# Layer 2's decay matrix: maxima broadcast by a load from DRAM scratch and masked on GpSimd, gate logarithms taken by tokens

## The chip, the core and the metric

The kernel runs on one core of a Trainium2 chip. The metric is device time in microseconds (us) of one execution; a lower number is better. TensorE (PE in the profile, with its weight loads as PEld) multiplies matrices, VectorE (DVE) and ScalarE (ACT) work on elements, GpSimd (POOL) does the same more slowly and issues some DMAs, SyncE (SP) issues the weight DMAs. Each engine takes its own instructions strictly in order; where one waits for a semaphore, everything behind it on that engine waits too.

## The reference, cut to what matters

A decoder trunk of two layers for 256 tokens of width 1024, in float32: layer 1 of the program is sparse attention, layer 2 is an mLSTM mixer with 8 heads (key width 128, value width 256). Layer 2's core, with input gate `i_pre` and forget gate `log_f` per token and head:

```
i_pre = gi + gate_b[0];  log_f = log_sigmoid(gf + gate_b[1])
b = cumsum(log_f);  log_d[j,s] = b[j] - b[s] + i_pre[s]  for s <= j, else -inf
m_j = max over s of log_d[j,s]
S = (q k^T) * exp(log_d - m_j);  num = S v;  den = sum of S
h = num / max(|den|, exp(-m_j))
```

The reference works in chunks of 64 tokens. The kernel uses the whole-sequence form of the same thing: with F the running sum of log_f, G = i_pre - F and M the running maximum of G, the decay factor of a key s and a query j is exp(G[s] - M[j]), and the floor of the denominator is exp(-(M + F)).

## The kernel before, in words

Keys of a decay matrix lie on the 128 partitions. For each head `DT[:, h]` has 384 columns: 256 for the first 128 keys against all queries, and 128 for the second 128 keys against the second 128 queries. In both, one 128x128 square is triangular.

Most of the program is the streamed projection of tokens: a weight block of 128x1024 is loaded by SP into one of 10 `raw` buffers (L86), ScalarE rounds it to a high part `wh` (L164), VectorE subtracts to get the low part `wl` (L169), and TensorE makes three products of each (hi·hi, lo·hi, hi·lo). There are 6 pairs of `wh`/`wl`, so the splits run some five blocks ahead of TensorE. In layer 2 a `tok_unit` of 512 columns takes four blocks (L548 to L550, 12 matmuls of 512 columns for each), a `ws_unit` two (L1611 to L1613, 24 matmuls of 256 columns for each).

The order of instructions on each engine is set by a scheduler that models the engines when the program is built; a region marked high priority goes ahead of other work as soon as the model finds its inputs ready. What is `pin`ned stays in the order of the text.

Layer 2 begins with the gate columns: 16 columns of a product (8 input gates, 8 forget gates, tokens on partitions) are copied to `GT` (L1240). Then, at high priority:

- four TensorE transposes bring `GT` to 8 rows of 256 tokens (L1332), and VectorE adds the biases (L1333, L1334);
- the log-sigmoid is computed on these 8x256 rows by three ScalarE functions and some VectorE operations (L1335 to L1343), then the running sum and maximum by scans (L1344, L1346), and -M is put in `nM` in two float32r parts (L1347 to L1349);
- two transposes bring G to columns (L1351), copied to `GF` (L1352);
- for every head, a matmul of a selector column with `nM` broadcasts -M over the partitions (L1357), two bf16 matmuls add the triangular mask (L1358, L1359), and two ScalarE exponentials with bias G write `DT` out of the PSUM bank (L1360, L1361).

Later the floor exp(-(M + F)) is made on rows (L1363 to L1365) and transposed by two more TensorE instructions (L1368).

The convolutions over q and k follow: each `conv_unit` is one `ws_unit`, a ScalarE pass out of PSUM (L1380), six VectorE taps (L1385) and a SiLU (L1387); by a rule in the text the SiLUs are issued behind the last decay exponential. `rows` shares its buffer with `QK`, into which the SiLUs write. Heads (L1392 on) use `DT` much later.

Of the kernel before, what the change touches and what calls it, by code (L numbers as in the profile page):

```python
# [23 lines left out]
class Kernel:  # L24
# [225 lines left out]
    def setup(self):  # L250
# [53 lines left out]
        self.identr = self.T(self.p1, [P, P], F32R)
        nc.vector.tensor_copy(self.identr, self.ident)
        nc.vector.tensor_copy(self.selh[0:8], self.ident[0:8, 0:8])

    def late_constants(self):
# [3 lines left out]
        m32 = self.T(self.p1, [P, P])  # L312
        g.memset(m32, 0.0)
        g.affine_select(m32, m32, pattern=[[1, P]], compare_op=OP.is_ge, fill=-1e30, base=0, channel_multiplier=-1)
        g.tensor_copy(self.mask, m32)
        g.tensor_copy(self.identb, self.ident)

    def small_loads(self):
        nc, t = self.nc, self.t
        self.first_small = [(self.pca[:, 32:89], t["second"])]  # L320
        self.small = [(self.bif, t["gate_b"]), (self.pcb, t["mixer"]), (self.compress, t["compress"])]
# [770 lines left out]
    def turn(self):  # L1092
# [146 lines left out]
        for a in range(2):  # L1239
            nc.vector.tensor_copy(GT[:, a], bs[a][:, 256:272])  # L1240
# [41 lines left out]
    def layer2(self):  # L1282
# [18 lines left out]
        mask, identb, selh = self.mask, self.identb, self.selh  # L1301
# [19 lines left out]
        rows = self.T(p2, [8, 9, SEQ], tag="QK")  # L1321
        gi, xf, e, u, sp, d, ones, Fc, M = [rows[:, n] for n in range(9)]
        nM = self.T(p2, [P, 384], F32R)
        GF = self.T(p2, [P, 2, 2, 8])
        g.memset(ones, 1.0)
        g.memset(nM.bitcast(F32), 0.0)
        bg, bt = self.bank(2), self.bank(3)
        with self.tc.high_priority():
            for a in range(2):
# [6 lines left out]
            nc.scalar.activation(e, e, AF.Exp, scale=-1.0)
            nc.vector.tensor_scalar(u, e, 1.0, None, op0=OP.add)
            nc.scalar.activation(sp, u, AF.Ln)
            nc.vector.scalar_tensor_tensor(d, u, -1.0, e, op0=OP.add, op1=OP.subtract)
            nc.vector.reciprocal(u, u)  # L1340
            nc.vector.tensor_tensor(d, d, u, op=OP.mult)
            nc.vector.tensor_sub(sp, sp, d)
            nc.vector.scalar_tensor_tensor(sp, xf, 0.0, sp, op0=OP.min, op1=OP.subtract)  # L1343
            nc.vector.tensor_tensor_scan(Fc, ones, sp, 0.0, OP.mult, OP.add)  # L1344
            nc.vector.tensor_sub(gi, gi, Fc)
            nc.vector.tensor_tensor_scan(M, ones, gi, 0.0, OP.mult, OP.max)  # L1346
            nc.vector.tensor_scalar(nM[0:8, 0:SEQ], M, -1.0, None, op0=OP.mult)  # L1347
            nc.vector.scalar_tensor_tensor(nM[32:40, 0:SEQ], M, -1.0, nM[0:8, 0:SEQ].bitcast(F32), op0=OP.mult, op1=OP.subtract)
            nc.vector.tensor_copy(nM[0:40, SEQ:384], nM[0:40, P:SEQ].bitcast(F32))  # L1349
            for a in range(2):  # L1350
                nc.tensor.transpose(bt[:, 8 * a : 8 * a + 8], gi[:, a * P : a * P + P], ident[:8, :8])  # L1351
            nc.vector.tensor_copy(GF[:, 0].rearrange("p a h -> p (a h)"), bt[:, 0:16])  # L1352
        DT = self.T(p2, [P, 8, 384], tag="DT")
        with self.tc.high_priority():
            for h in range(8):
                b = self.bank(2 + h % 2)
                nc.tensor.matmul(b[:, 0:384], selh[:, h : h + 1].to_broadcast([P, P]), nM, start=True, stop=False, skip_group_check=True)  # L1357
                nc.tensor.matmul(b[:, 0:P], identb, mask, start=False, stop=False, skip_group_check=True)  # L1358
                nc.tensor.matmul(b[:, SEQ:384], identb, mask, start=False, stop=True, skip_group_check=True)  # L1359
                nc.scalar.activation(DT[:, h, 0:SEQ], b[:, 0:SEQ], AF.Exp, bias=GF[:, 0, 0, h : h + 1])  # L1360
                last = nc.scalar.activation(DT[:, h, SEQ:384], b[:, SEQ:384], AF.Exp, bias=GF[:, 0, 1, h : h + 1])  # L1361
        v_unit(2, 2)
        nc.vector.tensor_tensor(M, M, Fc, op=OP.add)  # L1363
        nc.vector.tensor_scalar(M, M, -88.0, None, op0=OP.max)
        last = nc.scalar.activation(M, M, AF.Exp, scale=-1.0)  # L1365
        b = self.bank(2)
        for a in range(2):
# [328 lines left out]
```

## Time and profile before

| what | value |
|---|---|
| median of 3 runs | 427.54 us (427.27 to 427.9) |
| span of the profiled execution | 425.8 us |
| own time of the profiled execution | not listed apart from its span; the median lies 1.74 us above the span |
| PE busy | 415.7 us, 98% of the span |
| DVE, ACT, POOL busy | 353.7 us (83%), 272.0 us (64%), 82.1 us (19%) |
| granted TensorE clock | 0.999 |
| DMA | 94.54 MB, mean 222 GB/s |

The span runs from the first to the last instruction. A row of a timeline gives the start, the duration, the engine, the line, the operation and its operands (output first), and in brackets how long the engine was idle before and what ended it. Matmuls are pipelined: a 256-column matmul lasts 0.28 us but the next starts 0.12 us later, so what an instruction costs TensorE is read from the distance of starts. A row of windows gives busy time of each engine in a stretch, then the granted clock, the share of DMA engines busy and GB/s.

### The profile page before, as it was taken

The numbers are of one execution on the slowest core, as the hardware profiler recorded it, in microseconds if no ns is written. First come the engines' busy times: TensorE is split into PE (matmuls) and PEld (weight loads), VectorE is DVE, ScalarE is ACT, GpSimd is POOL, SyncE is SP. The second block draws the span as 40 slices with busy tenths as digits, with TensorE's granted clock in tenths as the row PEclk, the third lists the DMA queues.
The fourth block names the chain that finished last, engine by engine and source line by source line (L and its number), as shares of the span: only waits on it lengthen the run. The fifth ranks groups of instructions, "written<-read, shape, count | busy, mean of one in ns | idle before, by whom it ended". The sixth has DMA issues, their size and how long they took to land.

```text
span 425.8 us, 7641 instructions
## 1 busy us (share of the span) xinstructions
PE 415.7 (98%) x2701; PEld 359.7 (84%) x2701; DVE 353.7 (83%) x747; ACT 272.0 (64%) x542; POOL 82.1 (19%) x127
## 2 busy tenths in 40 slices
PE   7999999999999999999999999999999999999994
PEld 4899998789778878888998899888888888888884
DVE  6999798999999998979983796889878997458553
ACT  5766693788978964668576865465456454555523
POOL 4000212364586740120000000000000350220000
PEclk9999999999999999999999999999999999999999
DMA  8999986973799678148754366558555687540002
GB/s 313 413 408 407 396 306 192 357 280 107 256 353 391 226 255 307 58 145 295 247 172 168 105 237 190 166 174 264 163 188 197 213 290 229 168 142 0 2 0 99
DMA packets 26886, 94.54 MB, mean 222 GB/s; under 512 B 3072, under 2 KB 3088, under 8 KB 26848
## 3 DMA queue, kind: packets, MB, share of 16 engines
q1 hardware_dynamic: 26208, 92.30, 61.6%
q0 software_dynamic: 352, 0.97, 0.7%
q10 hardware_dynamic: 288, 0.79, 0.5%
q8 instruction: 21, 0.34, 0.3%
q14 instruction: 17, 0.14, 0.1%
HBM read 93.00 MB, written 1.05 MB: 221 GB/s over the span
## 4 chain that ended last, share of the span: by engine, by line
PE 86%; issue 6%; DMA 2%; POOL 2%; DVE 2%; ACT 1%; SPq 1%; DVEq 0%; POOLq 0%; ACTq 0%
PE bank L550 10%; PE bank L548 10%; PE bank L549 10%; PE bank L442 8%; PE bank L1613 6%; PE bank L1611 6%; PE bank L1612 6%; PE bank L1524 5%; PE bank L1045 5%; PE bank L1167 3%; DMA Q<-in_columns 2%; PE bank L808 2%; PE bank L1404 2%; PE bank L825 2%; PE bank L763 2%
## 5 line engine op out<-in xcount | busy, mean ns | idle before, releaser
L169 DVE TENSOR_TENSOR wl<-raw,wh 128x1024 fp32r<-128x1024 f32 (+4 forms) x127 | 139.3, 1112 | 37.3 <-ACT wh L164 36.4
L164 ACT ACTIVATE wh<-raw 128x1024 fp32r<-128x1024 f32 (+4 forms) x127 | 119.4, 957 | 72.9 <-PE bank L550 31.8
L548 PE MATMUL bank<-wh,one 128*128 128x512 f32 (+1 forms) x208 | 76.8, 370 | 0.0
L549 PE MATMUL bank<-wl,one 128*128 128x512 f32 (+1 forms) x208 | 76.3, 367 | 0.0
L550 PE MATMUL bank<-wh,one 128*128 128x512 f32 (+1 forms) x208 | 76.3, 368 | 0.0
L1611 PE MATMUL bank<-one,wh 128*128 128x256 f32 x208 | 59.6, 287 | 0.0
L1613 PE MATMUL bank<-one,wl 128*128 128x256 f32 x208 | 59.2, 285 | 0.1
L1612 PE MATMUL bank<-one,wh 128*128 128x256 f32 x208 | 59.0, 284 | 0.0
L803 POOL TENSOR_SCALAR Pr<-Pr,f 128x128 f32<-128x128 f32 (+1 forms) x42 | 46.7, 1130 | 31.4 <-DVE f L797 25.1
L548 PEld LDWEIGHTS bank<-wh,one 128*128 128x128 f32 x208 | 39.2, 189 | 6.1 <-DVE tz L520 0.2
L550 PEld LDWEIGHTS bank<-wh,one 128*128 128x128 f32 x208 | 39.2, 188 | 6.1
L549 PEld LDWEIGHTS bank<-wl,one 128*128 128x128 f32 x208 | 39.2, 189 | 5.9
L1611 PEld LDWEIGHTS bank<-one,wh 128*128 128x128 f32 x208 | 39.7, 191 | 1.3 <-issue 0.8
L1613 PEld LDWEIGHTS bank<-one,wl 128*128 128x128 f32 x208 | 39.7, 191 | 0.5 <-DVE wl L169 0.3
L1612 PEld LDWEIGHTS bank<-one,wh 128*128 128x128 f32 x208 | 39.7, 191 | 0.1
L789 ACT ACTIVATE Pr<-Pr,mn 128x128 f32<-128x128 f32 (+1 forms) x64 | 28.2, 444 | 4.4 <-DVE mn L782 4.4
L442 PE MATMUL bank<-one,wh 128*128 128x256 f32 x224 | 29.8, 284 | 0.7 <-ACT one L416 0.4
L442 PEld LDWEIGHTS bank<-one,wh 128*128 128x128 f32 x224 | 28.1, 192 | 1.1 <-ACT one L416 0.6
L1487 POOL DMA_DIRECT2D DT<-in_final_g x1 | 0.6, 560 | 131.7 <-DVE pl L1399 131.7
L160 POOL TENSOR_TENSOR raw<-raw,gate 128x256 f32<-128x256 f32 x16 | 15.5, 976 | 47.8 <-DMA raw<-in_out_b 22.5
L1385 DVE SCALAR_TENSOR_TENSOR conv<-bank,one,conv 128x255 f32<-128x255 f32 (+2 forms) x48 | 20.2, 471 | 2.1 <-ACT conv L1380 2.1
L861 DVE CUSTOM_DVE_ANT_0 raw<-raw,one,one 128x1024 f32<-128x1024 f32 x16 | 21.1, 1331 | 0.0
(343 smaller groups left out, 813.6 us busy)
## 6 DMA issues: line engine op xcount, KB each, us to landing
raw<-in_wide SPq DMA_DIRECT2D x44, 512.0 KB, 4.1
raw<-in_units SPq DMA_DIRECT2D x18, 512.0 KB, 3.5
raw<-in_turn SPq DMA_DIRECT2D x16, 512.0 KB, 7.7
raw<-in_gates SPq DMA_DIRECT2D x16, 512.0 KB, 4.7
raw<-in_out_b SPq DMA_DIRECT2D x16, 512.0 KB, 3.8
raw<-in_start SPq DMA_DIRECT2D x8, 512.0 KB, 9.6
Q<-in_columns SPq DMA_DIRECT2D x8, 512.0 KB, 9.6
raw<-in_hidden SPq DMA_DIRECT2D x8, 512.0 KB, 4.2
```

Source lines behind the costliest of these rows:

```text
L164: self.nc.scalar.activation(v(hi), src, AF.Copy)
L169: self.nc.vector.tensor_sub(v(lo), src, v(hi).bitcast(F32))
L442: nc.tensor.matmul(out, w[:, ch * P : ch * P + P], h[:, kk], start=(kk == 0 and m == 0 and ch % 2 == 0), stop=(kk == 7 and m == 2), skip_g ...
L548: nc.tensor.matmul(out, self.hh[:, kk, sl], wh, start=first, stop=False, skip_group_check=True)
L549: nc.tensor.matmul(out, self.hh[:, kk, sl], wl, start=False, stop=False, skip_group_check=True)
L550: nc.tensor.matmul(out, self.hl[:, kk, sl], wh, start=False, stop=last, skip_group_check=True)
L789: nc.scalar.activation(v, v, AF.Exp, bias=mn[:, a, br, j : j + 1], scale=-1.0, accum_out=sm[:, a, br, j : j + 1])
L803: es[br].tensor_scalar(v, v, F[n][:, a, br, j : j + 1], None, op0=OP.mult)
L1045: ins = nc.tensor.matmul(out, l[:, sl], w[:, c0:c1], start=(k == 0 and m == 0), stop=(k == N - 1 and m == 2), skip_group_check=True)
L1611: nc.tensor.matmul(out, wh, self.hh[:, kk], start=first, stop=False, skip_group_check=skip)
L1612: nc.tensor.matmul(out, wh, self.hl[:, kk], start=False, stop=False, skip_group_check=skip)
L1613: nc.tensor.matmul(out, wl, self.hh[:, kk], start=False, stop=last, skip_group_check=skip)
```

## The change

1. The biases are added by tokens: `bif` is now 128x16 (broadcast when loaded), and the copy of the gate columns becomes an addition.
2. The log-sigmoid of the forget gates is computed on `GT` itself, 128 partitions by 16 values, before the transposes: nine GpSimd operations, two ScalarE functions and one VectorE reciprocal in a chain. The two transposes of forget gates wait for it.
3. G and -M (now one float32 part) are stored by GpSimd DMAs to DRAM scratch (`store`, `shelf`). G comes back as columns by four small loads and a 32x32-block transpose on VectorE; -M is broadcast over the partitions by one load of 128x3072 floats into `DT`.
4. The mask is laid over both triangular squares of all heads by two GpSimd selects, and sixteen ScalarE exponentials run in place on `DT`. The selector, the bf16 mask and the bf16 identity are gone, with the 24 matmuls.
5. The floor is made by GpSimd and ScalarE on rows, and comes to columns by a store, four loads and a block transpose, in place of two TensorE transposes.

The new tile `shelf` is 8x384 and `store` 2x8x256 floats, in DRAM. Line numbers of the changed kernel are 9 lower for the code ahead of the change (L1167 is L1158, L548 is L539) and 1 lower behind it (L1380 is L1379, L1611 is L1610).

```diff
-            nc.vector.tensor_copy(GT[:, a], bs[a][:, 256:272])
+            nc.vector.tensor_tensor(GT[:, a], bs[a][:, 256:272], self.bif, op=OP.add)
...
-        nM = self.T(p2, [P, 384], F32R)
+        lf, e, u, sp, d = GT[:, :, 8:16], small[:, 0], small[:, 1], small[:, 2], small[:, 3]
+        nM = self.T(p2, [8, 384])
+        DT = self.T(p2, [P, 8, 384], tag="DT")
...
         with self.tc.high_priority():
+            g.tensor_scalar(d, lf, 0.0, 2.0, op0=OP.min, op1=OP.mult)
+            g.tensor_tensor(d, d, lf, op=OP.subtract)
+            nc.scalar.activation(e, d, AF.Exp)
+            g.tensor_scalar(u, e, 1.0, None, op0=OP.add)
+            nc.scalar.activation(sp, u, AF.Ln)
+            g.tensor_scalar(d, u, -1.0, None, op0=OP.add)
+            g.tensor_tensor(d, d, e, op=OP.subtract)
+            nc.vector.reciprocal(u, u)
+            g.tensor_tensor(d, d, u, op=OP.mult)
+            g.tensor_scalar(lf, lf, 0.0, None, op0=OP.min)
+            g.tensor_tensor(lf, lf, d, op=OP.add)
+            g.tensor_tensor(lf, lf, sp, op=OP.subtract)
             for a in range(2):
                 for n in range(2):
                     c = n * SEQ + a * P
                     nc.tensor.transpose(bg[0:8, c : c + P], GT[:, a, 8 * n : 8 * n + 8], ident)
...
+            nc.vector.tensor_copy(xf, bg[0:8, SEQ:])
+            nc.vector.tensor_copy(gi, bg[0:8, 0:SEQ])
+            nc.vector.tensor_tensor_scan(Fc, ones, xf, 0.0, OP.mult, OP.add)
             nc.vector.tensor_sub(gi, gi, Fc)
             nc.vector.tensor_tensor_scan(M, ones, gi, 0.0, OP.mult, OP.max)
+            nc.vector.tensor_scalar(nM[:, 0:SEQ], M, -1.0, None, op0=OP.mult)
+            nc.vector.tensor_copy(nM[:, SEQ:384], nM[:, P:SEQ])
+            pin(g.dma_start(store[0], gi))
+            pin(g.dma_start(shelf, nM))
+            for n in range(4):
+                pin(g.dma_start(blocks[32 * n : 32 * n + 16], store[0].rearrange("h (a k) -> (h a) k", a=2)[:, 32 * n : 32 * n + 32]))
+            pin(g.dma_start(DT.rearrange("p h q -> p (h q)"), shelf.rearrange("h q -> (h q)").unsqueeze(0).partition_broadcast(P)))
+            nc.vector.transpose(GF[:, 0:2].rearrange("p w h a -> p (w h a)"), blocks)
+            for half in (DT[:, :, 0:P], DT[:, :, SEQ:384]):
+                pin(g.affine_select(half, half, pattern=[[0, 8], [1, P]], compare_op=OP.is_ge, fill=-1e30, base=0, channel_multiplier=-1))
+            pin(g.tensor_tensor(M, M, Fc, op=OP.add))
+            g.tensor_scalar(M, M, -88.0, None, op0=OP.max)
+            nc.scalar.activation(M, M, AF.Exp, scale=-1.0)
             for h in range(8):
-                b = self.bank(2 + h % 2)
-                nc.tensor.matmul(b[:, 0:384], selh[:, h : h + 1].to_broadcast([P, P]), nM, start=True, stop=False, skip_group_check=True)
-                nc.tensor.matmul(b[:, 0:P], identb, mask, start=False, stop=False, skip_group_check=True)
-                nc.tensor.matmul(b[:, SEQ:384], identb, mask, start=False, stop=True, skip_group_check=True)
-                nc.scalar.activation(DT[:, h, 0:SEQ], b[:, 0:SEQ], AF.Exp, bias=GF[:, 0, 0, h : h + 1])
-                last = nc.scalar.activation(DT[:, h, SEQ:384], b[:, SEQ:384], AF.Exp, bias=GF[:, 0, 1, h : h + 1])
+                nc.scalar.activation(DT[:, h, 0:SEQ], DT[:, h, 0:SEQ], AF.Exp, bias=GF[:, 0, h, 0:1])
+                last = nc.scalar.activation(DT[:, h, SEQ:384], DT[:, h, SEQ:384], AF.Exp, bias=GF[:, 0, h, 1:2])
+            g.dma_start(store[1], M)
+            for n in range(4):
+                g.dma_start(blocks2[32 * n : 32 * n + 16], store[1].rearrange("h (a k) -> (h a) k", a=2)[:, 32 * n : 32 * n + 32])
+            nc.vector.transpose(GF[:, 2:4].rearrange("p w h a -> p (w h a)"), blocks2)
```

How the instructions stand, at three places. First TensorE at the opening of layer 2, before the change; L1332 are the four transposes of the gate columns (`one_519` is `GT`, `one_16` the identity), L1167 the products around them:

```order
L1167 MATMUL bank_2443<-wh_2309,one_6_69 128x272 x3
L1167 MATMUL bank_2443<-wh_2281,one_6_69 128x272 x2
L1167 MATMUL bank_2478<-wl_2476,one_4_68 128x512 x2
L1332 MATMUL bank_2635<-one_16_87,one_519_2555 8x128 x4
L1167 MATMUL bank_2478<-wh_2588,one_4_68 128x512 x2
L1167 MATMUL bank_2478<-wh_2588,one_6_69 128x512 x2
```

TensorE in the changed kernel, in the first `tok_unit` of layer 2, 27 of its 512-column matmuls in; L1341 are the transposes (`one_511` is `GT`), L539 to L541 what was L548 to L550:

```order
L541 MATMUL bank_2696<-wh_2703,one_6_71 128x512
L539 MATMUL bank_2695<-wh_2709,one_4_70 128x512
L540 MATMUL bank_2695<-wl_2710,one_4_70 128x512
L541 MATMUL bank_2695<-wh_2709,one_6_71 128x512
L1341 MATMUL bank_2632<-one_16_89,one_511_2545 8x128 x3
L539 MATMUL bank_2695<-wh_2709,one_4_70 128x512
L540 MATMUL bank_2695<-wl_2710,one_4_70 128x512
L541 MATMUL bank_2695<-wh_2709,one_6_71 128x512
```

One of the four transposes stays at its old place; the three others have moved behind these 27 matmuls.

Second, ScalarE where the decay exponentials stand, before the change (L164 is a weight split, L1380 a convolution's pass, L1365 the floor, L1360 and L1361 the exponentials of one head):

```order
L1380 ACTIVATE conv_2962<-bank_2901,one_21_99 128x256 x2
L1365 ACT_TABLE_LOAD
L1365 ACTIVATE QK_2630<-QK_2630 8x256
L164 ACTIVATE wh_3003<-raw_2740 128x1024
L1360 ACTIVATE DT_2661<-bank_2662,one_538_2632 128x256
L1361 ACTIVATE DT_2661<-bank_2662,one_538_2632 128x128
L1360 ACTIVATE DT_2661<-bank_2668,one_538_2632 128x256
L1361 ACTIVATE DT_2661<-bank_2668,one_538_2632 128x128
L164 ACTIVATE wh_3044<-raw_2746 128x1024
```

And in the changed kernel, where `wh_2981` is the block that was `wh_3003`, and `wh_3022` the one that was `wh_3044`:

```order
L1379 ACTIVATE conv_2940<-bank_2879,one_21_101 128x256 x2
L164 ACTIVATE wh_2981<-raw_2725 128x1024
L1362 ACT_TABLE_LOAD
L1362 ACTIVATE DT_2626<-DT_2626,one_536_2625 128x256 x8
L1363 ACTIVATE DT_2626<-DT_2626,one_536_2625 128x128 x8
L164 ACTIVATE wh_3022<-raw_2731 128x1024
L1360 ACTIVATE QK_2620<-QK_2620 8x256
L164 ACTIVATE wh_3052<-raw_2749 128x1024
L164 ACTIVATE wh_3094<-raw_2767 128x1024
L1386 ACT_TABLE_LOAD
```

All sixteen exponentials now stand in one piece ahead of the split of `wh_3022`, and the floor and the first SiLU come behind them.

Third, GpSimd in the changed kernel, behind the bias load of the last gate (before the change the next instruction there was the load of `final_g`); `one_528` holds d, e, u and sp, `one_511` is `GT`:

```order
L1582 DMA one_798_4109<-in_ada_b 1x16x64
L1326 TENSOR_SCALAR one_528_2621<-one_511_2545 128x16
L1327 TENSOR_TENSOR one_528_2621<-one_528_2621,one_511_2545 128x16
L1335 TENSOR_SCALAR one_511_2545<-one_511_2545 128x2x8
L1329 TENSOR_SCALAR one_528_2621<-one_528_2621 128x16
L1331 TENSOR_SCALAR one_528_2621<-one_528_2621 128x16
L1332 TENSOR_TENSOR one_528_2621<-one_528_2621 128x16
L1334 TENSOR_TENSOR one_528_2621<-one_528_2621 128x16
L1336 TENSOR_TENSOR one_511_2545<-one_511_2545,one_528_2621 128x2x8
L1337 TENSOR_TENSOR one_511_2545<-one_511_2545,one_528_2621 128x2x8
L1350 DMA store_2628<-QK_2620 8x256
L1351 DMA shelf_2627<-one_530_2622 8x384
```

Behind the last row stand the four small loads (L1353), the load of `DT` (L1354), the two selects (L1357), two operations for the floor (L1358, L1359) and its five DMAs (L1364, L1366).

More of the change, by code (lines that the diff above doesn't have):

```diff
@@ L320, in small_loads @@
         self.first_small = [(self.pca[:, 32:89], t["second"])]
[L321 removed]
+        self.small = [(self.bif, t["gate_b"].partition_broadcast(P)), (self.pcb, t["mixer"]), (self.compress, t["compress"])]
     def layer1(self):
@@ L1320, in layer2 @@
             values(a, slice(0, 2), vs[a].rearrange("p (h d) -> p h d", h=2))
-        rows = self.T(p2, [8, 9, SEQ], tag="QK")
-        gi, xf, e, u, sp, d, ones, Fc, M = [rows[:, n] for n in range(9)]
-        nM = self.T(p2, [P, 384], F32R)
-        GF = self.T(p2, [P, 2, 2, 8])
+        rows = self.T(p2, [8, 5, SEQ], tag="QK")
+        gi, xf, ones, Fc, M = [rows[:, n] for n in range(5)]
+        small = self.T(p2, [P, 5, 2, 8])
+        lf, e, u, sp, d = GT[:, :, 8:16], small[:, 0], small[:, 1], small[:, 2], small[:, 3]
+        nM = self.T(p2, [8, 384])
+        blocks, blocks2 = [self.T(p2, [P, 32]) for _ in range(2)]
+        GF = self.T(p2, [P, 4, 8, 2])
+        DT = self.T(p2, [P, 8, 384], tag="DT")
+        shelf = self.pd.tile([8, 384], F32, name=self.nm("shelf"), tag="shelf")
+        store = self.pd.tile([2, 8, SEQ], F32, name=self.nm("store"), tag="store")
         g.memset(ones, 1.0)
-        g.memset(nM.bitcast(F32), 0.0)
-        bg, bt = self.bank(2), self.bank(3)
+        g.memset(blocks, 0.0)
+        g.memset(blocks2, 0.0)
+        bg = self.bank(2)
         with self.tc.high_priority():
+            g.tensor_scalar(d, lf, 0.0, 2.0, op0=OP.min, op1=OP.mult)
[10 more added lines that the diff above has]
+            g.tensor_tensor(lf, lf, sp, op=OP.subtract)
             for a in range(2):
@@ L1339, in layer2 @@
[L1339 to L1344, printed above, removed]
+            nc.vector.tensor_copy(xf, bg[0:8, SEQ:])
+            nc.vector.tensor_copy(gi, bg[0:8, 0:SEQ])
@@ L1345, in layer2 @@
+            nc.vector.tensor_tensor_scan(Fc, ones, xf, 0.0, OP.mult, OP.add)
             nc.vector.tensor_sub(gi, gi, Fc)
             nc.vector.tensor_tensor_scan(M, ones, gi, 0.0, OP.mult, OP.max)
[L1347 to L1351, printed above, removed]
@@ L1362, in layer2 @@
-        v_unit(2, 2)
[L1363 to L1367, printed above, removed]
-            nc.tensor.transpose(b[:, 8 * a : 8 * a + 8], M[:, a * P : a * P + P], ident[:8, :8])
-        nc.vector.tensor_copy(GF[:, 1].rearrange("p a h -> p (a h)"), b[:, 0:16])
+            nc.vector.tensor_scalar(nM[:, 0:SEQ], M, -1.0, None, op0=OP.mult)
@@ L1669, in layout @@
         np.stack([w2[0], w2[0]], axis=2).reshape(P, 256), w2[1].reshape(P, 128)], axis=1)
-    out["gate_b"] = a["b_gate_b"][0].T
+    out["gate_b"] = a["b_gate_b"][0].reshape(1, 16)
     columns = a["ada_w"][0][:, : 2 * D].reshape(D, 2, KC, P).transpose(2, 1, 3, 0)
```

26 lines of the change are left out of this document (4 added, 22 removed).

## The prediction

> **What bounds the kernel now.** I read the page's busy line and its chain first, then the windows around layer 2's opening, then timelines.
>
> ```profile
> PE 415.7 (98%) x2701; PEld 359.7 (84%) x2701; DVE 353.7 (83%) x747; ACT 272.0 (64%) x542; POOL 82.1 (19%) x127
> PE 86%; issue 6%; DMA 2%; POOL 2%; DVE 2%; ACT 1%; SPq 1%; DVEq 0%; POOLq 0%; ACTq 0%
> 203.40:218.00 14.60, 14.60 (x122) 14.42 (x121) 13.93 (x28) 8.21 (x11) 0.00 (x0) 1.00 0.71 236
> 218.00:231.50 13.50, 13.50 (x108) 12.24 (x107) 6.97 (x10) 9.74 (x21) 0.00 (x0) 1.00 0.48 157
> 237.00:260.00 23.00, 23.00 (x177) 22.27 (x176) 20.09 (x37) 17.11 (x26) 0.00 (x0) 1.00 0.54 181
> ```
>
> TensorE is busy for 98% of the span and makes 86% of the chain that ended last. In the stretches where the decay matrix is made (203 to 231 us) and in the one behind it TensorE is busy for the whole of the stretch, at a granted clock of 1.00, while the other engines and the DMAs have room. So a matmul that goes from this place takes its time off the end, unless TensorE comes to wait for something new.
>
> **What goes: TensorE's own work.** The cost of an inserted instruction is the distance of starts around it, less what the neighbours need by themselves.
>
> ```profile
> 225.74 0.28 PE L1611 MATMUL bank<-one,wh 128*128 128x256 f32 x1
> 225.86 0.28 PE L1612 MATMUL bank<-one,wh 128*128 128x256 f32 x1
> 225.98 0.34 PE L1357 MATMUL bank<-one,one 128*128 128x384 f32 x1
> 226.16 0.23 PE L1358 MATMUL bank<-one,one 128*128 128x128 bf16 x1
> ...
> 226.25 0.37 PE L1613 MATMUL bank<-one,wl 128*128 128x256 f32 x1
> 226.46 0.28 PE L1611 MATMUL bank<-one,wh 128*128 128x256 f32 x1
> ...
> 212.05 0.28 PE L1611 MATMUL bank<-one,wh 128*128 128x256 f32 x1
> 212.26 0.29 PE L1351 MATMUL bank<-one,QK 8*128 8x8 f32 x2
> 212.48 0.38 PE L1612 MATMUL bank<-one,wh 128*128 128x256 f32 x1
> 212.70 0.28 PE L1613 MATMUL bank<-one,wl 128*128 128x256 f32 x1
> ...
> 235.22 0.39 PE L548 MATMUL bank<-wh,one 128*128 128x512 f32 x1
> 235.45 0.39 PE L549 MATMUL bank<-wl,one 128*128 128x512 f32 x1
> 235.77 0.29 PE L1368 MATMUL bank<-one,QK 8*128 8x8 f32 x2
> 235.98 0.50 PE L550 MATMUL bank<-wh,one 128*128 128x512 f32 x1
> 236.32 0.40 PE L548 MATMUL bank<-wh,one 128*128 128x512 f32 x1
> ...
> 186.63 0.60 PE L1332 MATMUL bank<-one,one 128*8 128x128 f32 x4
> 186.98 0.94 PE L1167 MATMUL bank<-wh,one 128*128 128x512 f32 x3
> ```
>
> - Undisturbed, 256-column matmuls start 0.12 us apart (225.74, 225.86), 512-column ones 0.23 (235.22, 235.45).
> - One head's decay group: from 225.86 to 226.46 pass 0.60 us, of which two steps of 0.12 are the neighbours' own; 0.36 us for a group, 8 x 0.36 = 2.88 us.
> - The two pairs of small transposes: (212.70 - 212.05) - 2 x 0.12 = 0.41 us, and (236.32 - 235.45) - 2 x 0.23 = 0.41 us; 0.82 us together.
> - What is split: the four gate transposes cost 186.98 - 186.63 = 0.35 us in one piece, hardly less than the two of L1351 do. So nearly all of it is paid for the interruption. As one and three they are two interruptions: 0.36 us more, between 0 and 0.41.
>
> TensorE's account is 2.88 + 0.82 - 0.36 = 3.34 us less.
>
> **What is added in front of TensorE: the gate logarithms.** The three late transposes wait for the last of nine GpSimd operations, and all the products behind them wait too.
>
> ```profile
> 186.36 0.17 DVE L1240 COPY one<-bank 128x16 f32<-128x16 f32 x1 [1.26 <-PE bank L1167]
> 186.82 1.23 DVE L169 TENSOR_TENSOR wl<-raw,wh 128x1024 fp32r<-128x1024 f32 x1 [0.29 <-ACT wh L164]
> ...
> 188.59 0.37 ACT L1296 ACTIVATE V<-bank 128x256 fp32r<-128x256 f32 x1
> 190.22 1.28 ACT L1336 ACT_TABLE_LOAD   x1
> ...
> 198.66 0.39 PE L548 MATMUL bank<-wh,one 128*128 128x512 f32 x1
> ...
> L297 POOL TENSOR_TENSOR PcT<-PcT,one 128x256 f32<-128x256 f32 x2 | 1.2, 617 | 0.0
> 147.14 2.92 POOL L803 TENSOR_SCALAR Pr<-Pr,f 128x256 f32<-128x256 f32 x1
> 148.14 1.21 DVE L169 TENSOR_TENSOR wl<-raw,wh 128x1024 fp32r<-128x1024 f32 x1
> 149.28 0.68 DVE L834 TENSOR_TENSOR y<-bank,xT 128x512 f32<-128x512 f32 x1
> ```
>
> `GT` is complete at 186.5. By the order, TensorE comes to the three transposes where the 28th of the first unit's matmuls stood, at 198.66, less some 0.1 for the three that left: 198.6. The chain has 12 us. In it ScalarE's first exponential stands behind the V copy that ends at 188.96 and a table load of 1.28: 190.5. Two splits of 1.06 (the L164 row below), a second load and the logarithm follow: 194.6. VectorE's reciprocal stands behind two subtractions (1.2 each) of those splits, at some 194.7. Three GpSimd operations are left. A GpSimd operation on 256 columns takes 0.62 us with VectorE quiet (L297); on 16 I take 0.3 with its handing over, 195.8 in all, 2.8 us before TensorE arrives.
>
> The row of 147.14 says what can go wrong. This operation has no more columns than L297, but lasted 2.92 us, until 150.06, and for two thirds of that VectorE worked on operations with two inputs in SBUF, the last being the L169 of 148.14. It came free when VectorE went on to L834, which reads PSUM. So a GpSimd operation can be kept waiting by a run of L169s, and two L169s back to back stand behind the reciprocal, too: 2.4 us. One such miss brings the chain to 198.2 to 198.5, still just in time; two misses make it 201 (a stall of 2.4). I allow 0.2 us, between 0 and 2.4.
>
> The Trainium skill has a rule for this row (SBUF — State Buffer, Who interferes with whom): VectorE with two SBUF inputs and GpSimd reading SBUF exclude each other, for the whole instruction. The trace agrees at 147.14. Taken at its worst, an estimate by that page, each of the nine operations would wait for a whole L169, and the sum would be the far end of the first rival below, 429.5.
>
> **What is added off TensorE: the broadcast, the mask, the exponentials.** Their cover is the lead of the weight splits.
>
> ```profile
> 225.51 1.06 ACT L164 ACTIVATE wh<-raw 128x1024 fp32r<-128x1024 f32 x1 [1.26 <-issue]
> ...
> one<-in_ada_b POOLq DMA_DIRECT2D x1, 4.0 KB, 2.4
> DT<-in_final_g POOLq DMA_DIRECT2D x1, 512.0 KB, 4.9
> L298 POOL TENSOR_SCALAR_AFFINE_SELECT PcT<-PcT 128x256 f32<-128x256 f32 x2 | 1.0, 527 | 0.0
> L314 POOL TENSOR_SCALAR_AFFINE_SELECT one<-one 128x128 f32<-128x128 f32 x1 | 0.8, 772 | 0.1
> 226.48 0.47 ACT L1360 ACTIVATE DT<-bank,one 128x256 f32<-128x256 f32 x1
> 226.85 0.36 ACT L1361 ACTIVATE DT<-bank,one 128x128 f32<-128x128 f32 x1
> 227.10 0.48 ACT L1360 ACTIVATE DT<-bank,one 128x256 f32<-128x256 f32 x1
> 228.97 0.40 PE L548 MATMUL bank<-wh,one 128*128 128x512 f32 x1
> ```
>
> - Rows of maxima: transposes at 198.9, then seven VectorE operations on 256 columns or fewer (0.68 for 512 columns in L834, so some 0.4 each) between four subtractions of 1.2 us: `nM` at about 207, an estimate.
> - Stores and loads: a small load by GpSimd's queue lands in 2.4 us, 512 KB in 4.9, so 2.5 us are for the bytes. The scratch lands at 210 to 212.5. The load of `DT` moves 1.5 MB, between 4.9 us (if bytes cost nothing more) and 14.7 (three times the whole); by the two rows 2.4 + 3 x 2.5 = 9.9. `DT` is there at about 221.5 (215.5 to 228). The DMAs are busy for 71% and 48% there.
> - Selects: 1024 elements for each of 128 partitions, two of them. By L298 (256 elements in 0.53) 2.1 us each; by L314, disturbed, 8 x 0.77 = 6.2. I take 2.1: 223.6 and 225.7.
> - Exponentials: 0.37 and 0.25 us apart. Eight long ones from 223.6, eight short ones from 226.6: all are done at 228.6 (up to 242.4 with both high ends).
>
> Behind them on ScalarE is queued the split of `wh_3022`, the fourth block of the `tok_unit` that starts at 228.97. Four blocks of 12 x 0.23 = 2.8 us bring the need for it to 228.97 + 8.3 + 1.1 (the two groups and the pair in between) = 238.3, less 3.3 saved: 235. Its two halves take 1.06 and 1.2, so ScalarE has to start by 232.7. The margin is 4 us: no cost. The small loads' block transpose makes VectorE wait some 3 us at about 212; it is idle for 6.5 us of the window from 218 and its splits lead by as much. The floor's store lands around 234, so the first SiLU starts about where it did, and the heads come only behind the convolutions. I count these at nothing, and all of them hang on the same lead.
>
> **The sum.** -3.34 + 0.2 = -3.1 us: span 425.8 - 3.1 = 422.7, and with the 1.74 us between span and median, 424.4 us. By its own terms this case reaches from 423.7 (the split costs nothing, no stall) to 425.5.
>
> **The rivals.**
>
> - *The logarithms hold TensorE.* If two of the last three GpSimd operations each lose to a run of subtractions, TensorE stands 2.4 us at the transposes: 427.54 - 3.34 + 2.4 = 426.6. At the far end each of the nine takes 1.2 in place of 0.3 us, the chain ends 8.1 us later, at 203.9, TensorE stands 5.3 us, and the time is 429.5. For it: the 2.92 us row. Against it: each subtraction follows a ScalarE split, and where ScalarE waits for the chain, VectorE has nothing to subtract. Chance 0.12: 0.06 for a loss small enough to leave more than 0.2%, 0.04 for about the 2.4 us, 0.02 for the far end.
> - *The decay comes too late (slower).* With the high ends, the exponentials end at 242.4 and TensorE waits 9.7 us for `wh_3022`: 427.54 - 3.34 + 9.7 = 433.9. It begins to cost at 232.7, and the kernel is slower than before from 236 on, 7.5 us later than I reckon. For it: a chain of four DMAs and selects that no row shows at this size. Chance 0.09.
> - *No change.* Something that isn't TensorE (weights, say) sets the pace behind 237 and takes the saving up: 427.5. Against it: TensorE is busy for all of that window, DMA share 0.54. Chance 0.05.
>
> **How the numbers follow.** The forecast keeps 0.74. About 0.2% (0.86 us) is what a measurement of this kernel can tell from no change. Faster: 0.74 + 0.06 = 0.80; same: 0.04 + 0.05 = 0.09; slower: 0.02 + 0.09 = 0.11. The range goes from 423.6 past the first rival's 426.6 to 427.0; it leaves out the second rival, the third, the first's far end and a little below, some 0.18.
>
> **What would show it.** Right: no matmul between the weight products where L1357 stood; the start of the first product of the later stages (the `tok_unit` of 228.97, the first head) about 3 us earlier; TensorE idle by under 0.5 us at L1341; the last decay exponential before 232. Wrong: PE idle at L1341 released by POOL L1337 (first rival); ScalarE idle before L1362 well beyond 225 and PE waiting for `wh` at about 235 (second); the early stages 3 us earlier but the end not (third).

## The result, and the profile after

The changed kernel takes 424.29 us (median of 5 runs, 423.6 to 424.41), beside 427.31 us (427.23 to 427.9) for the kernel before on the same chip: a ratio of 0.9919 with a 95% interval of 0.9907 to 0.9932. The profiled execution took 424.37 us with a span of 422.6 us, against 425.8 us before.

The page of the changed kernel, its busy line and its chain:

```profile
PE 412.3 (98%) x2673; PEld 357.3 (85%) x2673; DVE 349.9 (83%) x737; ACT 271.1 (64%) x541; POOL 95.5 (23%) x149
PE 81%; DMA 7%; issue 5%; POOL 2%; DVE 2%; SPq 1%; ACT 1%; DVEq 0%; POOLq 0%
```

The same three windows as before (the columns are the stretch, the busy time of PE, PEld, DVE, ACT and POOL with their instructions, the granted clock, the DMA share and GB/s):

```profile
203.40:218.00 14.60, 14.60 (x120) 14.46 (x119) 11.45 (x21) 7.74 (x11) 3.51 (x7) 1.00 0.82 276
218.00:231.50 13.50, 13.50 (x98) 12.73 (x97) 7.21 (x11) 12.36 (x23) 6.63 (x8) 1.00 0.50 175
237.00:260.00 23.00, 23.00 (x190) 22.80 (x189) 20.39 (x35) 14.11 (x20) 0.00 (x0) 1.00 0.67 210
```

TensorE has 28 instructions and 3.4 us of busy time fewer and is as full as before in each window; GpSimd has 13.4 us more of it. The DMAs' larger share of the chain (7% beside 2%) comes from the loads of `in_columns` at the start of the program, between 4 and 35 us, ahead of all that was changed. Nothing new stands beside TensorE in layer 2: the bound there is the same, with less in it.

Where the time went is read from two marks: the first product of layer 2's opening, and the first product of the last stage. The view of one line's instructions gives them ("first start to last start"). Before:

```profile
L1167 PE MATMUL bank<-wh,one x64: 282/388/478, 172.9 to 190.0; 128*128 128x272 f32 x32, 128*128 128x512 f32 x32
L1524 PE MATMUL bank<-wh,QK x30: 276/392/476, 397.0 to 419.0; 128*128 128x512 f32 x18, 128*128 128x256 f32 x12
```

After:

```profile
L1158 PE MATMUL bank<-wh,one x64: 282/388/497, 173.3 to 190.3; 128*128 128x272 f32 x32, 128*128 128x512 f32 x32
L1523 PE MATMUL bank<-wh,QK x30: 276/392/481, 393.8 to 415.8; 128*128 128x512 f32 x18, 128*128 128x256 f32 x12
```

From mark to mark pass 224.1 us before and 220.5 us after: 3.6 us less. The span shrank by only 3.2 because this execution reached layer 2 0.4 us later; over all executions shown here that first mark lies between 172.2 and 173.3, with code ahead of it that the change leaves nearly as it was. Behind the second mark both have 28.8 us. So the distance between the marks is the finest measure of this change, and is used below beside the times. It comes from one execution of each kernel; four of them that do the same work on TensorE with the same relative places of its operands (the changed kernel and three below) all have 220.5, so I take it as good to about 0.2 us.

### The profile page after: what moved, and what is told of

The parts are those of the page before. It is cut to its first block, busy times and chain, and to the rows that moved or that the text cites. A ratio compares the mean times of both kernels' runs of the same rounds, so it can differ in the third digit from the quotient of the medians.

```text
span 422.6 us, 7599 instructions
## 1 busy us (share of the span) xinstructions
PE 412.3 (98%) x2673; PEld 357.3 (85%) x2673; DVE 349.9 (83%) x737; ACT 271.1 (64%) x541; POOL 95.5 (23%) x149
## 4 chain that ended last, share of the span: by engine, by line
PE 81%; DMA 7%; issue 5%; POOL 2%; DVE 2%; SPq 1%; ACT 1%; DVEq 0%; POOLq 0%
PE bank L539 10%; PE bank L541 10%; PE bank L540 10%; PE bank L1612 6%; PE bank L1610 6%; PE bank L1611 6%; PE bank L1523 5%; PE bank L1036 5%; DMA Q<-in_columns 5%; PE bank L433 3%; PE bank L1158 3%; DMA KH<-in_columns 2%; PE bank L799 2%; PE bank L1403 2%; PE bank L816 2%
## 5 line engine op out<-in xcount | busy, mean ns | idle before, releaser
L164 ACT ACTIVATE wh<-raw 128x1024 fp32r<-128x1024 f32 (+4 forms) x127 | 119.1, 957 | 69.6 <-PE bank L541 32.4
L539 PE MATMUL bank<-wh,one 128*128 128x512 f32 (+1 forms) x208 | 77.0, 370 | 0.0
L541 PE MATMUL bank<-wh,one 128*128 128x512 f32 (+1 forms) x208 | 76.1, 367 | 0.0
L1610 PE MATMUL bank<-one,wh 128*128 128x256 f32 x208 | 59.6, 287 | 0.0
L1611 PE MATMUL bank<-one,wh 128*128 128x256 f32 x208 | 58.8, 283 | 0.0
L541 PEld LDWEIGHTS bank<-wh,one 128*128 128x128 f32 x208 | 39.2, 188 | 6.2
L539 PEld LDWEIGHTS bank<-wh,one 128*128 128x128 f32 x208 | 39.2, 189 | 6.1 <-DVE tz L511 0.2
L1610 PEld LDWEIGHTS bank<-one,wh 128*128 128x128 f32 x208 | 39.7, 191 | 1.3 <-issue 0.8
L1611 PEld LDWEIGHTS bank<-one,wh 128*128 128x128 f32 x208 | 39.8, 191 | 0.1
```

The costliest lines, as they stand in the source:

```text
L164: self.nc.scalar.activation(v(hi), src, AF.Copy)
L539: nc.tensor.matmul(out, self.hh[:, kk, sl], wh, start=first, stop=False, skip_group_check=True)
L541: nc.tensor.matmul(out, self.hl[:, kk, sl], wh, start=False, stop=last, skip_group_check=True)
L1610: nc.tensor.matmul(out, wh, self.hh[:, kk], start=first, stop=False, skip_group_check=skip)
L1611: nc.tensor.matmul(out, wh, self.hl[:, kk], start=False, stop=False, skip_group_check=skip)
```

## The experiments

Each time is a median with its range; the kernel before ran on the same chip beside each group, with medians of 427.31 beside the changed kernel and of 427.98, 427.43 and 427.51 beside the three groups of experiments, so that times of two groups are compared by their ratios to it. "Marks" is the distance just described (before 224.1, after 220.5).

### The matmuls put back

The changed kernel with the 24 matmuls of the decay back in TensorE's stream, on data that nobody needs:

```diff
...
+            nc.vector.tensor_copy(old[0:8], nM)
+            for h in range(8):
+                b = self.bank(2 + h % 2)
+                nc.tensor.matmul(b[:, 0:384], pick[:, h : h + 1].to_broadcast([P, P]), old, start=True, stop=False, skip_group_check=True)
+                nc.tensor.matmul(b[:, 0:P], zero, zero, start=False, stop=False, skip_group_check=True)
+                nc.tensor.matmul(b[:, SEQ:384], zero, zero, start=False, stop=True, skip_group_check=True)
+                nc.vector.tensor_copy(tip[:, h : h + 1], b[:, 0:1])
```

> The changed kernel with the 24 matmuls of the decay put back as dead work: same shapes, banks and pairing, on zeros and on -M, each bank read by one small VectorE copy; the decay itself still comes from the load. If the gain is TensorE's own time (8 groups of 0.36 us), the time rises by 2.8 us over the changed kernel, to 427.1 (426.6 to 427.6). If the gain came from the work taken off VectorE and ScalarE or from the earlier decay, these are kept here and the time stays within 1 us of 424.3.

Measured: 426.8 us (426.55 to 427.05, 9 runs), ratio to before 0.9972 (0.9963 to 0.9982); marks 223.4, 2.9 more than after. By the times less is back, 2.5 us between the medians and 2.3 between the ratios, whose intervals allow for 1.3 to 3.2. The scheduler put the groups in pairs. One pair in the timeline of TensorE:

```profile
207.97 0.28 PE L1624 MATMUL bank<-one,wh 128*128 128x256 f32 x1
208.09 0.34 PE L1359 MATMUL bank<-one,one 128*128 128x384 f32 x1
...
208.72 0.36 PE L1625 MATMUL bank<-one,wh 128*128 128x256 f32 x1
208.92 0.28 PE L1626 MATMUL bank<-one,wl 128*128 128x256 f32 x1
```

From 207.97 to 208.92 pass 0.95 us, of which two steps of 0.12 are the neighbours' own: 0.71 for a pair, four times 2.84. The step behind the interruption (208.72 to 208.92) is itself 0.08 too long, so one must count to the second start behind it. The decay itself is still made by the load, GpSimd and ScalarE in this kernel, and still 2.9 of the 3.6 us are gone: that part of the gain was TensorE's own time.

### The mask alone

The kernel before with the broadcast still a matmul; the mask goes to GpSimd, behind a ScalarE pass that adds the bias, and the exponentials run in place:

```diff
...
-                nc.tensor.matmul(b[:, 0:P], identb, mask, start=False, stop=False, skip_group_check=True)
-                nc.tensor.matmul(b[:, SEQ:384], identb, mask, start=False, stop=True, skip_group_check=True)
-                nc.scalar.activation(DT[:, h, 0:SEQ], b[:, 0:SEQ], AF.Exp, bias=GF[:, 0, 0, h : h + 1])
-                last = nc.scalar.activation(DT[:, h, SEQ:384], b[:, SEQ:384], AF.Exp, bias=GF[:, 0, 1, h : h + 1])
+                nc.scalar.activation(DT[:, h, 0:SEQ], b[:, 0:SEQ], AF.Identity, bias=GF[:, 0, 0, h : h + 1])
+                nc.scalar.activation(DT[:, h, SEQ:384], b[:, SEQ:384], AF.Identity, bias=GF[:, 0, 1, h : h + 1])
+            for half in (DT[:, :, 0:P], DT[:, :, SEQ:384]):
+                g.affine_select(half, half, pattern=[[0, 8], [1, P]], compare_op=OP.is_ge, fill=-1e30, base=0, channel_multiplier=-1)
+            for h in range(8):
+                last = nc.scalar.activation(DT[:, h], DT[:, h], AF.Exp)
```

> The kernel before with the mask alone moved: the broadcast stays a matmul of 384 columns for each head, ScalarE writes it to SBUF with the bias added, GpSimd masks, and ScalarE takes the exponentials in place; only the 16 bf16 matmuls go. Theory (TensorE's time is what counts): the broadcast matmul alone needs some 0.16 us and an interruption, so 0.10 to 0.15 of the 0.36 us of a group go, 0.8 to 1.2 us in all, 426.3. If the cost of a group is the interruption and not its columns, under 0.4 us goes, 427.0.

Measured: 426.18 us (425.95 to 426.4, 5 runs), ratio 0.9959 (0.9946 to 0.9971); marks 222.5, 1.6 less than before, where 0.8 to 1.2 had been expected. TensorE at two of the broadcasts:

```profile
217.67 0.28 PE L1614 MATMUL bank<-one,wh 128*128 128x256 f32 x1
217.78 0.51 PE L1357 MATMUL bank<-one,one 128*128 128x384 f32 x2
218.13 0.28 PE L1615 MATMUL bank<-one,wl 128*128 128x256 f32 x1
218.25 0.28 PE L1613 MATMUL bank<-one,wh 128*128 128x256 f32 x1
```

Two broadcasts cost 218.25 - 217.67 - 2 x 0.12 = 0.34 us, 0.17 each, where a group with its masks cost 0.36. The two bf16 matmuls were over half of a group. So the gain of the decay's part splits about evenly, 1.5 us for the mask and 1.4 for the broadcast, and the 1.6 us measured leave no cost for what GpSimd and ScalarE took on here.

### The logarithms by rows

The changed kernel without the nine operations on `GT`; the four gate transposes stay in one piece at the old place, and the log-sigmoid runs on 8x256 rows, as before:

```diff
-            g.tensor_scalar(d, lf, 0.0, 2.0, op0=OP.min, op1=OP.mult)
...
-            g.tensor_tensor(lf, lf, sp, op=OP.subtract)
...
+            nc.scalar.activation(e, xf, AF.Abs)
+            nc.scalar.activation(e, e, AF.Exp, scale=-1.0)
...
+            nc.vector.scalar_tensor_tensor(sp, xf, 0.0, sp, op0=OP.min, op1=OP.subtract)
+            nc.vector.tensor_tensor_scan(Fc, ones, sp, 0.0, OP.mult, OP.add)
```

> The changed kernel with the gate logarithms made from 8x256 rows again, behind the transposes, on VectorE and ScalarE; broadcast, mask and floor as changed. The four gate transposes stand in one piece again, and the rows of maxima are ready some 8 to 10 us later. Theory (only TensorE's account counts, the decay has room): 0.2 to 0.4 us under the changed kernel, 424.0, since one interruption goes, with DT landing at about 228 and the exponentials done at about 236 and no wait of TensorE. Rival (the logarithms by tokens are needed to hide the broadcast): TensorE or the convolutions wait, 425.5 to 428.

Measured: 424.55 us (424.12 to 425.81, 5 runs), ratio 0.9925 (0.9911 to 0.9938), not to be told from the changed kernel; marks 220.7. GpSimd and ScalarE in it, at the selects (behind the load of `DT`) and the short decay exponentials:

```profile
225.68 2.14 POOL L1352 TENSOR_SCALAR_AFFINE_SELECT DT<-DT 128x1024 f32<-128x1024 f32 x2 [9.65 <-DMA DT<-shelf]
...
231.85 2.44 ACT L1358 ACTIVATE DT<-DT,one 128x128 f32<-128x128 f32 x8
```

All of the decay comes 6 to 8 us later than in the changed kernel (the last exponential ends at 234.3), and the time does not move: the scheduler knows of the lateness and puts three weight splits ahead of the exponentials. But the 0.2 to 0.4 us that the single interruption was expected to bring did not come either. The marks are 0.2 longer than after, and TensorE waits once, behind the scores of the first heads:

```profile
249.03 0.38 PE L1387 MATMUL bank<-QK 128*128 128x128 f32 x2
249.64 0.36 PE L539 MATMUL bank<-wh,one 128*128 128x256 f32 x1 [0.23 <-DVE conv L1379]
```

This product waits for VectorE's taps of a convolution (L1379). The changed kernel's trace shows no wait of TensorE between 190 and 395 us. So the lead that the logarithms by tokens buy may be worth a few tenths of a us, by this one execution, and nothing that the times can tell.

### The load made twice

```diff
             pin(g.dma_start(DT.rearrange("p h q -> p (h q)"), shelf.rearrange("h q -> (h q)").unsqueeze(0).partition_broadcast(P)))
+            pin(g.dma_start(DT.rearrange("p h q -> p (h q)"), shelf.rearrange("h q -> (h q)").unsqueeze(0).partition_broadcast(P)))
```

> The changed kernel with the load of the broadcast rows made twice in a row, the second over the first, so that the decay matrix is there some 9 us later (landing at about 228, the last exponential at about 236). Theory (the decay has lead, and the scheduler's order moves two or three weight splits ahead of it): within 0.4 us of the changed kernel, 424.3 to 424.7. Rival (the lead is used up at 232.7): 3.3 us more, about 427.6, with TensorE waiting for a weight block at about 235.

Measured: 424.62 us (424.13 to 425.63, 5 runs), ratio 0.9936 (0.9924 to 0.9949); marks 220.5. GpSimd and ScalarE:

```profile
218.96 0.53 POOL L1355 DMA_DIRECT2D DT<-shelf  x1 [9.17 <-DMA DT<-shelf]
228.51 2.14 POOL L1358 TENSOR_SCALAR_AFFINE_SELECT DT<-DT 128x1024 f32<-128x1024 f32 x2 [9.01 <-DMA DT<-shelf]
...
220.97 1.06 ACT L164 ACTIVATE wh<-raw 128x1024 fp32r<-128x1024 f32 x1 [1.82 <-PE bank L1612]
...
233.04 1.04 ACT L164 ACTIVATE wh<-raw 128x1024 fp32r<-128x1024 f32 x1
233.99 2.44 ACT L1364 ACTIVATE DT<-DT,one 128x128 f32<-128x128 f32 x8
```

The last exponential ends at 236.4, the point from which the late decay should have made the kernel slower than before; TensorE waited for nothing in the window from 203 to 270. The split that had to start by 232.7 now stands ahead of the exponentials, at 220.97 (counted in the order of the splits), and a later one (233.04) between the long and the short exponentials. The deadline belonged to one order of ScalarE's instructions, and the scheduler makes another when its model sees the delay. A lateness that the model does not see was not tried.

### One interruption in place of two, and what it brought to light

The columns of the gates are laid out so that two transposes of 40 columns do for four of 8:

```diff
-        GT = self.T(pc, [P, 2, 16])
+        GT = self.T(pc, [P, 2, 2, 32])
...
-                for n in range(2):
-                    c = n * SEQ + a * P
-                    nc.tensor.transpose(bg[0:8, c : c + P], GT[:, a, 8 * n : 8 * n + 8], ident)
+                nc.tensor.transpose(bg[0:40, a * P : a * P + P], GT[:, a].rearrange("p n w -> p (n w)")[:, 0:40], ident)
```

> The changed kernel with the gate columns laid out so that one transpose of 40 columns brings input and forget gates at once: two transposes in one piece in place of one and three. Theory: one interruption of 0.36 us and two transposes go, 0.3 to 0.5 us under the changed kernel, 423.9, seen in the trace as one gap between products instead of two. If TensorE already waits for the logarithms at the late transposes, the gap there is longer than 0.4 us and the time the same as the changed kernel's.

Measured: 425.34 us (424.92 to 426.11, 5 runs), ratio 0.9943 (0.993 to 0.9955); marks 222.7: 2.2 us longer than after, not shorter. Yet the interruption itself is short, in the timeline of TensorE:

```profile
198.41 0.39 PE L541 MATMUL bank<-wh,one 128*128 128x512 f32 x1
198.63 0.38 PE L1340 MATMUL bank<-one,one 128*40 128x128 f32 x2
...
199.09 0.39 PE L540 MATMUL bank<-wl,one 128*128 128x512 f32 x1
```

It costs 199.09 - 198.41 - 2 x 0.23 = 0.22 us. The loss is elsewhere: every 512-column product is a few ns slower. `GT` has grown by 384 bytes per partition, and all weight buffers lie that much higher in SBUF. Three kernels tell the address from the transposes. The first is the changed kernel with nothing but a tile of 384 bytes:

```diff
         GT = self.T(pc, [P, 2, 16])
+        nc.gpsimd.memset(self.T(pc, [P, 96]), 0.0)
```

> The changed kernel with nothing but an unused tile of 384 bytes per partition behind the gates' tile, so that every weight buffer lies 384 bytes higher, as in the kernel with one interruption. Theory (address): the 512-column products of layer 2 start 230 ns apart in place of 226.6, and the time is 1.3 to 1.8 us over the changed kernel, about 425.7. Rival (the padded gates or the 40-column transposes themselves did it): 226.6 ns, 424.3 as the changed kernel.

The same with 128 bytes (`[P, 32]`):

> The changed kernel with an unused tile of 128 bytes per partition. The weight buffers then start at 256 bytes of a 512-byte line, in place of 128. If only a start on a whole 512-byte line is slow: 424.3 as the changed kernel. If every start but that at 128 is slow: 230 ns a product and some 425.7.

And the kernel with one interruption, with 128 bytes of padding more:

```diff
         GT = self.T(pc, [P, 2, 2, 32])
+        nc.gpsimd.memset(self.T(pc, [P, 32]), 0.0)
```

> The kernel with one interruption and 128 bytes more of padding, so that the weight buffers lie 512 bytes higher than in the changed kernel, at the same place within 512 bytes. Address theory: products 226.6 ns apart again, and the two transposes in one piece bring 0.4 to 0.5 us: about 423.8, faster than both kernels. Rival (address has no part): 425.3 as the kernel with one interruption.

The address decides: 425.4 us (425.02 to 425.56, 5 runs; ratio 0.9948, 0.9936 to 0.996) and 425.37 us (425.12 to 426.82, 6 runs; 0.9955, 0.9943 to 0.9967) for the two shifts, and 423.85 us (423.53 to 423.96, 4 runs; 0.9912, 0.9899 to 0.9925) where the shift is undone. Three more kernels, of the changed kernel again, ask which address counts. The first two have a tile of 128 bytes ahead of the token matrix, the second has another of 128 bytes behind `GT`, and the third has one of 256 bytes behind `GT` alone:

```diff
+        gap = self.T(pc, [P, 32])
         self.hh = self.T(pc, [P, KC, SEQ], F32R)
...
```

> The changed kernel with an unused tile of 128 bytes per partition ahead of the two halves of the token matrix, so that these and the weight buffers all start at an even multiple of 128 bytes (in the changed kernel all start at an odd one). Rule 1 (the operand that streams through TensorE wants an odd multiple): 512-column products, which stream weights, 230 ns apart, and the 256-column products, which stream the token matrix, slower as well, by 2 to 4 ns each for some 960 of them: 427 to 429. Rule 2 (only the two operands' places against each other count): 226.6 ns and 424.3. Rule 3 (only the weights' place counts, as a place of its own): 425.4, with the 256-column products as before.

> The same tile of 128 bytes, and another behind the gates' tile, so that the token matrix starts at an even multiple of 128 bytes and the weights at an odd one (384 of 512). Rule 1: 512-column products at 226.6 ns, 256-column ones slower: 426 to 428. Rule 2: 512-column products at 230 ns, 425.4. Rule 3: 424.3.

> The changed kernel with an unused tile of 256 bytes behind the gates' tile: weights at 384 of 512 bytes, an odd multiple of 128, the token matrix where it was. If odd against even decides: 226.6 ns and 424.3 as the changed kernel. If only 128 of 512 is the quick place: 230 ns and 425.4.

Measured: 423.81 us (423.41 to 423.98, 4 runs; ratio 0.991, 0.9897 to 0.9922), 425.74 us (425.3 to 426.92, 6 runs; 0.9958, 0.9946 to 0.997) and 423.77 us (423.55 to 425.05, 6 runs; 0.9916, 0.9903 to 0.9929). The pace is read from the first `tok_unit` of layer 2, between two rows of TensorE's timeline that many products apart. The changed kernel, 25 steps:

```profile
193.05 0.39 PE L540 MATMUL bank<-wl,one 128*128 128x512 f32 x1
...
198.72 0.40 PE L541 MATMUL bank<-wh,one 128*128 128x512 f32 x1
```

Weights alone 384 bytes higher, 23 steps:

```profile
192.56 0.40 PE L539 MATMUL bank<-wh,one 128*128 128x512 f32 x1
...
197.91 0.40 PE L541 MATMUL bank<-wh,one 128*128 128x512 f32 x1
```

Its window there, in which the granted clock is 1.00:

```profile
192.00:198.00 6.00, 6.00 (x28) 4.85 (x27) 5.18 (x10) 5.53 (x8) 1.63 (x3) 1.00 0.93 325
```

Token matrix 128 and weights 256 bytes higher, 25 steps:

```profile
192.63 0.40 PE L542 MATMUL bank<-wl,one 128*128 128x512 f32 x1
...
198.45 0.40 PE L543 MATMUL bank<-wh,one 128*128 128x512 f32 x1
```

That is 226.8, 232.6 and 232.8 ns a step. All eight kernels together, the others read in the same way, with the start address of each operand, modulo 256 bytes, as the built program places it (a step is the distance of starts of two 512-column products):

| kernel | token matrix | weights | ns a step | marks | time |
|---|---|---|---|---|---|
| changed kernel | 128 | 128 | 226.8 | 220.5 | 424.29 |
| one interruption | 128 | 0 | 232.8 | 222.7 | 425.34 |
| weights 384 up | 128 | 0 | 232.6 | 222.6 | 425.4 |
| weights 128 up | 128 | 0 | 232.8 | 222.3 | 425.37 |
| one interruption, padded | 128 | 128 | 226.9 | 220.4 | 423.85 |
| weights 256 up | 128 | 128 | 226.7 | 220.5 | 423.77 |
| both 128 up | 0 | 0 | 226.9 | 220.5 | 423.81 |
| tokens 128 up, weights 256 up | 0 | 128 | 232.8 | 222.6 | 425.74 |

Of the three rules in the expectations only rule 2 fits all eight: products are quick where both operands start at the same place within 256 bytes, and about 2.6% slower where they lie 128 apart. Neither operand's own place counts. The padding moves every tile behind it together with the weights, so the weights were not moved apart from the buffers that are split into them, and only multiples of 128 bytes were tried. The kernel before and the changed kernel both have 128 and 128, so this has no part in the change's gain; a tile of another size could have taken 2 of the 3.6 us away.

The padded kernel with one interruption should have been 0.4 to 0.5 us under the changed kernel, and its marks are only 0.1 under. TensorE at the place of the first interruption, in the padded kernel, where no transpose stands there any more, with the weight load of the next product, which waits for a split (`wh`), and VectorE released by the same split:

```profile
186.18 0.62 PE L1158 MATMUL bank<-wl,one 128*128 128x512 f32 x2
186.88 1.42 PE L1158 MATMUL bank<-wh,one 128*128 128x512 f32 x5
...
186.88 1.22 PEld L1158 LDWEIGHTS bank<-wh,one 128*128 128x128 f32 x6 [0.50 <-ACT wh L164]
...
186.86 2.39 DVE L169 TENSOR_TENSOR wl<-raw,wh 128x1024 fp32r<-128x1024 f32 x2 [0.30 <-ACT wh L164]
```

The same place in the changed kernel:

```profile
186.56 0.63 PE L1158 MATMUL bank<-wl,one 128*128 128x512 f32 x2
187.03 0.27 PE L1341 MATMUL bank<-one,one 128*8 128x128 f32 x1
187.25 0.96 PE L1158 MATMUL bank<-wh,one 128*128 128x512 f32 x3
```

With the transpose 0.69 us pass, without it 0.70. The product behind needs a weight block whose high part is ready just then (its weight load waits for ScalarE's split until 186.88, and VectorE, which needs the same one, is released at 186.86). TensorE stands here for 0.70 - 2 x 0.23 = 0.24 us in any case, and one transpose put here is free. No kernel of this series is measurably faster than the changed one: the three quick ones at 423.8 have ratios of 0.991 to 0.9916, within its interval.

## Why the prediction was right, step by step

**The sum.** Forecast 424.4, measured 424.29; -3.1 us forecast, -3.0 by the medians and -3.6 between the marks. That the times agree to 0.1 us is luck: the interval of the ratio is 1.1 us wide, and the two kernels above that only add padding and keep the pace (weights 256 up, both 128 up) took 3.7 less than the kernel before on their chip. What was right is the mechanism, TensorE's own work; two cost terms were set too high, by 0.35 us together. By its own terms the low end of 423.7 would be 427.54 - 3.34 - 0.36 = 423.84, and the high end of 425.5 was not worked out.

**The decay groups, 8 x 0.36 = 2.88 us: right.** Putting the matmuls back costs 2.9 us.

**The two pairs of small transposes, 0.82 us: not tried alone.** With this price and 0.21 for the split (below) the parts come to -2.88 - 0.82 + 0.21 = -3.49, beside 3.6 between the marks; so the price fits, but no run takes these four alone.

**The gate transposes, +0.36 us: too much.** The step said that nearly all the cost of the four is for the interruption. The three late ones in the changed kernel's timeline:

```profile
198.72 0.40 PE L541 MATMUL bank<-wh,one 128*128 128x512 f32 x1
198.95 0.49 PE L1341 MATMUL bank<-one,one 128*8 128x128 f32 x3
...
199.52 0.40 PE L540 MATMUL bank<-wl,one 128*128 128x512 f32 x1
```

They cost 199.52 - 198.72 - 2 x 0.23 = 0.34 us, as reckoned. But the one at the old place costs nothing beside the wait for the split, as shown above. Before, the four stood on that wait, too (VectorE is released at 186.82 in the row shown with the forecast). The two products ahead of them began at

```profile
186.16 0.63 PE L1167 MATMUL bank<-wl,one 128*128 128x512 f32 x2
```

and 186.98 - 186.16 - 2 x 0.23 = 0.36 us, of which 0.24 was the wait. So the split costs 0.34 + 0.23 - 0.36 = 0.21 us. The prediction took the time from the transposes' start to the next product's as their price without asking whether that product was ready.

**The gate logarithms, 0.2 us of stall: none came, and the lock was smaller than feared.** GpSimd and VectorE in the changed kernel:

```profile
187.41 1.12 POOL L1327 TENSOR_TENSOR one<-one,one 128x16 f32<-128x16 f32 x1
188.62 1.10 POOL L1335 TENSOR_SCALAR one<-one 128x16 f32<-128x16 f32 x1
190.97 0.26 POOL L1329 TENSOR_SCALAR one<-one 128x16 f32<-128x16 f32 x1 [1.25 <-ACT one L1328]
...
195.41 1.19 POOL L1337 TENSOR_TENSOR one<-one,one 128x16 f32<-128x16 f32 x1
```

```profile
187.22 3.52 DVE L169 TENSOR_TENSOR wl<-raw,wh 128x1024 fp32r<-128x1024 f32 x3 [0.29 <-ACT wh L164]
...
195.30 2.39 DVE L169 TENSOR_TENSOR wl<-raw,wh 128x1024 fp32r<-128x1024 f32 x2 [0.63 <-ACT wh L164]
```

Three of the nine, all beside subtractions with two SBUF inputs, took 1.10 to 1.19 us; the others 0.22 to 0.30. The chain ended at 196.60 (195.8 forecast), 2.35 us before TensorE came. The forecast feared that a run of subtractions holds GpSimd to its end. Here it does not: the three of 187.22 last to 190.7, and inside them two GpSimd operations finished, at 188.5 and 189.7. Each lost about one subtraction, 0.9 us. The Trainium skill (SBUF — State Buffer, Who interferes with whom) has the lock as one for the whole instruction, and the trace agrees with that, by these rows; a run of instructions was not one lock here. The forecast's row of 147.14 lasted through two VectorE instructions all the same, and why GpSimd came in between them here and not there is open. The first rival at its far end, with all nine held, would have needed a subtraction under way at each.

**The broadcast, the mask, the exponentials: hidden, as forecast, and earlier.** The path in the changed kernel on GpSimd and ScalarE:

```profile
209.59 0.54 POOL L1354 DMA_DIRECT2D DT<-shelf  x1 [0.54 <-DMA shelf<-one]
219.06 3.13 POOL L1357 TENSOR_SCALAR_AFFINE_SELECT DT<-DT 128x1024 f32<-128x1024 f32 x2 [8.93 <-DMA DT<-shelf]
...
224.16 2.44 ACT L1363 ACTIVATE DT<-DT,one 128x128 f32<-128x128 f32 x8
226.50 1.04 ACT L164 ACTIVATE wh<-raw 128x1024 fp32r<-128x1024 f32 x1
...
231.58 1.15 ACT L1386 ACTIVATE QK<-conv 128x512 f32<-128x512 f32 x2
```

The DMA view, with the time from issue to landing at the end:

```profile
DT<-shelf POOLq DMA_DIRECT2D x1, 1536.0 KB, 9.4
```

The load took 9.4 us (9.9 forecast from two smaller loads), the two selects 3.1 (4.2; in the runs with a later decay 2.14 for both, so the price scaled from L298 was twice too high), and the split that had to start by 232.7 started at 226.50, where the forecast had 228.6. So the second rival was 6 us away. Two smaller points were off without cost: VectorE did not wait for the small loads (its block transpose at 212.95 shows no idle time), and the first SiLU came at 231.58, some 6 us earlier than before and not "about where it did".

**The rivals.** None came: no stall at the late transposes, no late decay, and the saving reached the last stage, as the 28.8 us behind the second mark on both sides show.

## What to carry to other kernels

Where one engine is busy for 98% of the span, price what leaves it by the distance of starts around it, to the second start behind; but look first whether the next instruction was ready, since a cost that covers a wait brings nothing when it is removed: the wait stays. Lead that is there already is worth little, and a scheduler can make more of it: delays of 6 and 10 us in the decay cost nothing that the times could tell, and once 0.23 us of waiting in the trace. And compare the pace of untouched matmuls ahead of believing any difference under 1%: a tile of another size moves every buffer behind it.

## What the runs showed of the hardware

Streams of 512-column float32r products, each with a weight load of its own, run at 226.8 ns a product where the stationary and the streamed operand start at the same place within 256 bytes of a partition, and at 232.7 where they lie 128 bytes apart, 2 us over layer 2 of this kernel (eight kernels, granted clock 1.00). The Trainium skill (TensorE: Matmul & The Clock Gate, Step-by-step: what each phase is for) says that loading the next weights takes no read bandwidth from the running matmul; these runs suggest that the two reads do touch, though what they share stays open. The 256-column products of layer 2 start 0.12 us apart in both kinds of kernel; they were not slowed.

Small matmuls put into a stream cost 0.17 us for each broadcast of 384 columns (among 256-column products), 0.22 us for two transposes of 40 columns and 0.34 for three of 8 (among 512-column products): 0.11 to 0.17 us for an instruction.
